# Splitting the load and the norm of x over two queues and two engines at the head of a one-core transformer block

## The chip, the cores and the metric

The kernel runs on one core of one Trainium2 chip. The metric is the device time of one execution in microseconds; the time of a kernel is the median of its runs.

## The reference, cut to what matters

The reference is one hybrid transformer layer over 256 tokens of width 1024 and a final norm: a state space mixer and a sparse attention side by side, then a mixture of 32 experts. Only its first lines matter here. A vector `c` gives shift and scale by a product with `w_ada`, the tokens `x` are normalized row by row, and the result goes into one wide projection:

```python
ada = jax.nn.silu(c) @ w_ada + b_ada
shift1, scale1, gate1, shift2, scale2, gate2 = [a[:, None, :] for a in jnp.split(ada, 6, axis=-1)]
hn = _rmsnorm(h, norm1_g) * (1.0 + scale1) + shift1     # x * rsqrt(mean(x * x) + eps) * g
... hn @ w_xbc, hn @ w_q, ...                             # w_in, 1024 x 9040
```

Everything is in float32.

## The kernel before

The work is one long program for the five engines, written stage by stage. A framework orders the instructions on each engine by its own estimate of when their inputs are ready, so the order on an engine can differ from that of the lines (in the timeline below, the load of x's first half stands ahead of the row loads that the program writes first).

**Loads.** All weights are a list, `stream`, issued in order on SyncE's queue (SP): for k = 0 to 7 first `ada{k}` (columns of `w_ada`, two transfers of 512 KB) and `sl{k}` (128 rows of `w_in`, 768 KB), then the rest. `slot` takes one of 19 buffers, `pump` issues as long as buffers are free, `release` gives one back.

**The front.** The tokens come in two halves of 128 rows, `Xv[:, 0]` and `Xv[:, 1]`, 512 KB each. `rows` loads `c`, `norm1_g` and `b_ada` as rows of a cleared tile `T1r`; TensorE turns it (L299) and ScalarE takes the columns (`th`, `T1`, L304, L305). GpSimd works out silu of c, `sc`. `warm` issues products that nobody reads: `WARM0` = 6 on the identity at the start and `WARM1` = 14 on `T1r` behind L299. One such product is two instructions in the trace.

**The norm.** The sums of squares of the two halves are formed on ScalarE (half 0, L331) and on VectorE (half 1, L328); both stand in `ssq`. A trial root on one element (L333) brings ScalarE's table for roots in early. `rsqrt` then treats both halves in one go: a root on ScalarE (L315), and on VectorE five small instructions (L316 to L320) that make the reciprocal and refine it. VectorE scales half 0 (L335), ScalarE half 1 (L336), into XN.

**The first projection.** For each k, `p0_rows` forms row k of shift and scale (16 instructions `ar<-ada,sc`), `p0_ab` turns it into columns, `xn_transposes` turns XN (four instructions for two k, L404, both halves of XN in each group) and copies it to XT, `p0_cols` makes the normalized input in two parts, HH and HL, `p0_split` makes the parts `wh` (ScalarE) and `wl` (VectorE) of the weight slice `sl{k}`, one half at a time, and `p0_mm` issues 18 products for each half. On TensorE the order is `p0_rows(0)`, `xn_transposes(0)`, four filling products on XT, `xn_transposes(1)`, `p0_mm(0, 0)`, and so on. Products of all helpers stand under L104 (`mm`), VectorE's under L87, L90, L94 and L95.

Of the kernel before, what the change touches and what calls it, by code (L numbers as in the profile page):

```python
# [12 lines left out]
AF = mybir.ActivationFunctionType  # L13
OP = mybir.AluOpType
# [4 lines left out]
D = 1024  # L19
# [3 lines left out]
EPS = 1e-6  # L23
# [5 lines left out]
WARM, WARMN = 1, 8  # L29
WN = 128  # L30
WARM0 = 6
WARM1 = 14
WARM2 = 1
WARM3 = 12
RATE_XB, RATE_ATTN, RATE_SSD = 1.15, 1.5, 1.35
# [22 lines left out]
def tile_hybrid_block(ctx: ExitStack, tc: tile.TileContext, x, c, positions, w_ada, b_ada, norm1_g, w_in, conv_w,  # L58
                      conv_b, dt_bias, a_log, d_skip, ssm_norm_g, w_ssm_out, cmp_pe_k, cmp_w1_k, cmp_w2_k, cmp_pe_v,
                      cmp_w1_v, cmp_w2_v, w_nsa_out, w_o, norm2_g, w_router_group, b_router_group, w_router_expert,  # L60
                      b_router_expert, w_exp_gate, w_exp_up, w_exp_down, final_g, out, dbg=None):
    nc = tc.nc
    PE, V, A, G, SP = nc.tensor, nc.vector, nc.scalar, nc.gpsimd, nc.sync
# [10 lines left out]
    def ps(b, name):  # L74
        return psp.tile([128, 512], F32, tag=f"b{b}", name=name)

    def work(shape, tag, name, bufs=1, dt=F32):
        return wk.tile(shape, dt, tag=tag, bufs=bufs, name=name)

    def const(shape, name, dt=F32):  # L80
        return csp.tile(shape, dt, name=name)

    def lasting(shape, name, dt=F32):
        return cst.tile(shape, dt, name=name)

    def stt(o, a, s, b, op0, op1):
        return V.scalar_tensor_tensor(o, a, s, b, op0=op0, op1=op1)  # L87

    def tt(o, a, b, op):
        return V.tensor_tensor(o, a, b, op=op)  # L90

    def ts(o, a, s1, op0, s2=None, op1=None):
        if op1 is None:
            return V.tensor_scalar(o, a, s1, None, op0=op0)  # L94
        return V.tensor_scalar(o, a, s1, s2, op0=op0, op1=op1)  # L95

    def warm(b, n):

        for _ in range(n):
            w = box["warm"]  # L100
            mm(b[:, 0:w.shape[1]], ident, w, True, True)
# [4 lines left out]
    def dram(ap, off, dims):  # L106
        return bass.AP(tensor=ap.tensor, offset=ap.offset + off, ap=dims)
# [14 lines left out]
    def slot(name):  # L122
        tag = free.pop(0)
        tag_of[name] = tag
        return (big if tag[0] == "s" else box["xtra"]).tile([128, 2048], F32, tag=tag, name=name)
# [11 lines left out]
    def keep(n):  # L137
        st["keep"] = n
        pump()
# [92 lines left out]
    T1r = work([128, 128], "w1k", "T1r", 4)  # L232
    V.memset(T1r, 0.0)

    def rows(q, dst, r0, src, n):
        q.dma_start(dst[r0:r0 + n, :], dram(src, 0, [[128, n], [1, 128]]))

    X = slot("X")
    Xv = X.rearrange("p (t d) -> p t d", t=2)
    rows(SP, T1r, 0, c, 8)  # L240
    rows(SP, T1r, 8, norm1_g, 8)
    rows(SP, T1r, 16, b_ada, 16)
    for i in range(2):
        SP.dma_start(Xv[:, i], x[0, i * 128:(i + 1) * 128, :])
    keep(4)


# [46 lines left out]
    epsc = lasting([128, 1], "epsc")  # L294
# [5 lines left out]
    box["warm"] = T1r  # L300
    warm(ps(6, "warm"), WARM1)
    T1 = const([128, 32], "T1")
    th = const([128, 8], "th")
# [8 lines left out]
    def rsqrt(o, ss, n, name):  # L312

        v, t = const([128, n], name + "v"), const([128, n], name + "t")
        A.activation(o, ss, AF.Sqrt, bias=epsc, scale=1.0 / D)  # L315
        ts(v, ss, 1.0 / D, OP.mult, EPS, OP.add)  # L316
        V.reciprocal(o, o)
        tt(t, o, o, OP.mult)
        stt(t, t, -0.5, v, OP.mult, OP.mult)
        stt(o, t, 1.5, o, OP.add, OP.mult)  # L320
# [1 line left out]

    XN = slot("XN")
    XNv = XN.rearrange("p (t d) -> p t d", t=2)
    ssq = const([128, 2], "ssq")
    for i in range(2):
        if i:
            V.tensor_tensor_reduce(out=XNv[:, i], in0=Xv[:, i], in1=Xv[:, i], scale=1.0, scalar=0.0, op0=OP.mult,  # L328
                                   op1=OP.add, accum_out=ssq[:, i:i + 1])
        else:  # L330
            A.activation(XNv[:, i], Xv[:, i], AF.Square, accum_out=ssq[:, i:i + 1])  # L331
    rx = const([128, 2], "rx")
    A.activation(rx[0:1, 0:1], th[0:1, 0:1], AF.Sqrt, scale=0.0, bias=epsc[0:1])  # L333
    rsqrt(rx, ssq, 2, "rx")
    ts(XNv[:, 0], Xv[:, 0], rx[:, 0:1], OP.mult)  # L335
    A.activation(XNv[:, 1], Xv[:, 1], AF.Copy, scale=rx[:, 1:2])  # L336
    XT = slot("XT")
    XTv = XT.rearrange("p (k t) -> p k t", k=8)
    HH, HL = slot("HH"), slot("HL")
# [1077 lines left out]
    def carve(t, *shapes):  # L1417

        at, r = 0, []
        for sh in shapes:  # L1420
            n = 1
            for k in sh:
                n *= k
            v, names = t[:, at:at + n], "abcde"[:len(sh)]
            at += n
            r.append(v.rearrange(f"p ({' '.join(names)}) -> p {' '.join(names)}",
                                 **dict(zip(names[1:], sh[1:]))) if len(sh) > 1 else v)
        return r
# [10 lines left out]
    hp, th, DTc, DTd = carve(scr2, (256,), (256,), (256,), (256,))  # L1439
# [396 lines left out]
    sf, vf, rf, rv, r_ = carve(rw_[:, 256:268], (2, 2), (2,), (2,), (2,), (2,))  # L1836
# [75 lines left out]
```

## Time and profile before

| | us |
|---|---|
| median of 3 runs | 681.53 |
| lowest and highest run | 680.92, 682.42 |
| the profiled execution | 683.83 |
| span of the profiled execution, first to last instruction | 682.1 |
| TensorE busy | 634.7 (93%) |
| VectorE busy | 468.3 (69%) |
| ScalarE busy | 324.7 (48%) |
| read from HBM | 190.98 MB |

Busy times are unions over the span; a matmul's end is modelled, so a busy TensorE is not one at its peak. In the rows further down, PE is TensorE's products, PEld its weight loads, DVE VectorE, ACT ScalarE, POOL GpSimd, SPq SyncE's queue of issues. A row of a timeline has the start, the duration, engine, line, operation, the tiles (written <- read), the shapes, a count, and in brackets the idle time before it and what ended it.

### The profile page before, as it was taken

The page shows a single profiled execution, that of the slowest core. Times are in us where ns is not written, and L with a number is a line of the kernel's source. Part 1 is how long each engine was busy: PE and PEld are TensorE (multiplying, and loading weights), DVE is VectorE, ACT ScalarE, POOL GpSimd, SP SyncE. Part 2 cuts the span into 40 slices and gives each one's busy share as a digit, 9 for nine tenths or more (in the row PEclk, how much of TensorE's full clock was granted, in tenths as well). Part 3 has the DMA queues.
Part 4 walks back from the last instruction along what each step waited for, and adds up shares of the span by engine and source line. Part 5 has one row for each costly group of instructions (what it writes and reads, how often), then busy time and mean ns, then how long its engine had stood idle before and what let it go on. Part 6 is the DMA issues. An engine that isn't in the chain of part 4 may idle for free. (4 is left out here: it accounts for less than half of the span.)

```text
span 682.1 us, 14140 instructions
## 1 busy us (share of the span) xinstructions
PE 634.7 (93%) x5610; PEld 500.9 (73%) x5611; DVE 468.3 (69%) x1158; ACT 324.7 (48%) x630; POOL 7.5 (1%) x67
## 2 busy tenths in 40 slices
PE   7999999899899999999999999998988999989873
PEld 6889889797767787898998999874646645655532
DVE  3657999995787878786899867565635634555635
ACT  4435878763358776463845544443223212223214
POOL 2000000000000000000000000000000000000000
PEclk9999999999989999999999999998998999999998
DMA  8997971478647767636395988656999999999992
GB/s 263 335 336 247 371 225 41 147 247 285 214 133 250 264 220 231 209 125 216 123 309 187 378 345 330 249 195 237 383 411 422 418 419 419 418 420 418 418 382 93
DMA packets 102196, 193.28 MB, mean 283 GB/s; under 512 B 7636, under 2 KB 83940, under 8 KB 90596
## 3 DMA queue, kind: packets, MB, share of 16 engines
q1 hardware_dynamic: 101268, 191.05, 77.4%
q8 instruction: 57, 0.93, 0.6%
q10 hardware_dynamic: 848, 1.11, 0.5%
q14 instruction: 23, 0.19, 0.1%
HBM read 190.98 MB, written 1.16 MB: 282 GB/s over the span
## 5 line engine op out<-in xcount | busy, mean ns | idle before, releaser
L104 PE MATMUL moe<-u,XG 128*32 128x256 f32 (+1 forms) x560 | 71.3, 381 | 3.3 <-SPq L1709 1.9
L104 PE MATMUL moe<-g,XG 128*32 128x256 f32 (+1 forms) x560 | 70.0, 380 | 2.5 <-PEq L1585 1.6
L104 PEld LDWEIGHTS moe<-g,XG 128*32 128x32 f32 (+1 forms) x560 | 38.3, 112 | 22.4 <-issue 10.0
L87 DVE SCALAR_TENSOR_TENSOR hp<-hp,moe 64x256 f32<-64x256 f32 x32 | 13.4, 419 | 47.0 <-ACT hp L1608 46.5
L104 PEld LDWEIGHTS moe<-u,XG 128*32 128x32 f32 (+1 forms) x560 | 35.7, 112 | 11.5 <-DMA u<-in_w_exp_up_dram 2.5
L104 PE MATMUL moe<-d,rw 128*32 128x512 f32 (+1 forms) x280 | 37.7, 617 | 2.0 <-ACT XG L1504 1.2
L1608 ACT ACTIVATE hp<-moe 64x256 f32<-64x256 f32 x32 | 12.1, 379 | 54.1 <-PEq L1585 31.3
L104 PE MATMUL pj_z<-HH,wl 128*128 128x256 f32 x128 | 37.1, 290 | 0.6 <-DVE wl L90 0.6
L104 PE MATMUL pj_z<-HH,wh 128*128 128x256 f32 x128 | 36.9, 288 | 0.0
L104 PE MATMUL pj_z<-HL,wh 128*128 128x256 f32 x128 | 36.7, 287 | 0.0
L104 PE MATMUL moe<-DT,HFh 128*128 128x256 f32 x128 | 32.0, 299 | 2.1 <-DVE DT L90 1.1
L1652 ACT ACTIVATE Y<-moe 128x512 fp32r<-128x512 f32 x15 | 9.0, 597 | 49.1 <-DVE moe L90 49.1
L913 ACT ACTIVATE P<-P,mn 128x128 f32<-128x128 f32 (+1 forms) x64 | 28.4, 446 | 5.4 <-DVE mn L910 5.3
L104 PE MATMUL moe<-DT,HFl 128*128 128x256 f32 x128 | 30.7, 289 | 0.2 <-DVE HFl L87 0.2
L1504 ACT ACTIVATE XG<-moe,GC 128x256 f32<-128x256 f32 x36 | 18.1, 564 | 25.6 <-PE moe L104 25.6
L104 PE MATMUL pj_xb<-HH,wh 128*128 128x256 f32 x96 | 27.0, 282 | 3.0 <-ACT BC L493 1.5
L104 PEld LDWEIGHTS moe<-DT,HFh 128*128 128x128 f32 x128 | 24.0, 196 | 5.8 <-issue 5.8
L104 PE MATMUL xa<-HH,wh 128*128 128x256 f32 x96 | 27.8, 293 | 0.0
L104 PE MATMUL pj_xb<-HH,wl 128*128 128x256 f32 x96 | 26.8, 279 | 0.0
L104 PE MATMUL pj_xb<-HL,wh 128*128 128x256 f32 x96 | 26.8, 279 | 0.0
L104 PEld LDWEIGHTS pj_z<-HH,wl 128*128 128x128 f32 x128 | 24.6, 192 | 2.9 <-issue 1.6
L104 PE MATMUL xa<-HL,wh 128*128 128x256 f32 x96 | 26.5, 280 | 0.0
(479 smaller groups left out, 2002.0 us busy)
## 6 DMA issues: line engine op xcount, KB each, us to landing
g<-in_w_exp_gate_dram SPq DMA_DIRECT2D x30, 1024.0 KB
u<-in_w_exp_up_dram SPq DMA_DIRECT2D x30, 1024.0 KB
d<-in_w_exp_down_dram SPq DMA_DIRECT2D x30, 1024.0 KB
ad<-in_w_ada_dram SPq DMA_DIRECT2D x16, 1024.0 KB
ada<-in_w_ada_dram SPq DMA_DIRECT2D x16, 512.0 KB
z<-in_w_in_dram SPq DMA_DIRECT2D x8, 1024.0 KB
so<-in_w_ssm_out_dram SPq DMA_DIRECT2D x8, 1024.0 KB
qk<-in_w_in_dram SPq DMA_DIRECT2D x8, 936.0 KB
```

The costliest lines, as they stand in the source:

```text
L87: return V.scalar_tensor_tensor(o, a, s, b, op0=op0, op1=op1)
L104: return PE.matmul(o, l, r, start=start, stop=stop)
L913: A.activation(o, o, AF.Exp, bias=mn[:, n:n + 1], scale=-1.0, accum_out=sm[:, n:n + 1])
L1504: A.activation(o, b_, AF.Identity, scale=GC[:, 1, k:k + 1], bias=GC[:, 0, k:k + 1])
L1608: A.activation(th[g], B4[g, s * 256:(s + 1) * 256], AF.Tanh, scale=0.5)
L1652: A.activation(R(Y[:, 0]), B6, AF.Copy)
```

## The change

The second half of x and the three row loads are issued by ScalarE's queue, x's first half stays on SP. Each half of x has a norm of its own: half 0 is squared and scaled by ScalarE; of half 1, ScalarE squares the first 512 columns and VectorE the others, an addition joins the sums, and VectorE scales the first 512 columns and ScalarE the others. `norm_of` is `rsqrt` for one column. The trial root covers two elements. `WARM1` goes from 14 to 9.

```diff
--- before.py
+++ after.py
@@ -29,7 +29,7 @@
 WARM, WARMN = 1, 8
 WN = 128
 WARM0 = 6
-WARM1 = 14
+WARM1 = 9
 WARM2 = 1
 WARM3 = 12
 RATE_XB, RATE_ATTN, RATE_SSD = 1.15, 1.5, 1.35
@@ -237,11 +237,11 @@
 
     X = slot("X")
     Xv = X.rearrange("p (t d) -> p t d", t=2)
-    rows(SP, T1r, 0, c, 8)
-    rows(SP, T1r, 8, norm1_g, 8)
-    rows(SP, T1r, 16, b_ada, 16)
-    for i in range(2):
-        SP.dma_start(Xv[:, i], x[0, i * 128:(i + 1) * 128, :])
+    SP.dma_start(Xv[:, 0], x[0, 0:128, :])
+    rows(A, T1r, 0, c, 8)
+    A.dma_start(Xv[:, 1], x[0, 128:256, :])
+    rows(A, T1r, 8, norm1_g, 8)
+    rows(A, T1r, 16, b_ada, 16)
     keep(4)
 
 
@@ -322,18 +322,29 @@
 
     XN = slot("XN")
     XNv = XN.rearrange("p (t d) -> p t d", t=2)
-    ssq = const([128, 2], "ssq")
-    for i in range(2):
-        if i:
-            V.tensor_tensor_reduce(out=XNv[:, i], in0=Xv[:, i], in1=Xv[:, i], scale=1.0, scalar=0.0, op0=OP.mult,
-                                   op1=OP.add, accum_out=ssq[:, i:i + 1])
-        else:
-            A.activation(XNv[:, i], Xv[:, i], AF.Square, accum_out=ssq[:, i:i + 1])
-    rx = const([128, 2], "rx")
-    A.activation(rx[0:1, 0:1], th[0:1, 0:1], AF.Sqrt, scale=0.0, bias=epsc[0:1])
-    rsqrt(rx, ssq, 2, "rx")
-    ts(XNv[:, 0], Xv[:, 0], rx[:, 0:1], OP.mult)
-    A.activation(XNv[:, 1], Xv[:, 1], AF.Copy, scale=rx[:, 1:2])
+    ssq, ssh = const([128, 2], "ssq"), const([128, 2], "ssh")
+    rx, rv, rt_ = const([128, 2], "rx"), const([128, 2], "rv"), const([128, 2], "rt_")
+
+    def norm_of(i):
+        o, v, t, q = (w[:, i:i + 1] for w in (rx, rv, rt_, ssq))
+        A.activation(o, q, AF.Sqrt, bias=epsc, scale=1.0 / D)
+        ts(v, q, 1.0 / D, OP.mult, EPS, OP.add)
+        V.reciprocal(o, o)
+        tt(t, o, o, OP.mult)
+        stt(t, t, -0.5, v, OP.mult, OP.mult)
+        stt(o, t, 1.5, o, OP.add, OP.mult)
+
+    A.activation(XNv[:, 0], Xv[:, 0], AF.Square, accum_out=ssq[:, 0:1])
+    A.activation(rx[0:1, 0:2], th[0:1, 0:2], AF.Sqrt, scale=0.0, bias=epsc[0:1])
+    norm_of(0)
+    A.activation(XNv[:, 0], Xv[:, 0], AF.Copy, scale=rx[:, 0:1])
+    A.activation(XNv[:, 1, 0:512], Xv[:, 1, 0:512], AF.Square, accum_out=ssh[:, 0:1])
+    V.tensor_tensor_reduce(out=XNv[:, 1, 512:1024], in0=Xv[:, 1, 512:1024], in1=Xv[:, 1, 512:1024], scale=1.0,
+                           scalar=0.0, op0=OP.mult, op1=OP.add, accum_out=ssh[:, 1:2])
+    tt(ssq[:, 1:2], ssh[:, 0:1], ssh[:, 1:2], OP.add)
+    norm_of(1)
+    ts(XNv[:, 1, 0:512], Xv[:, 1, 0:512], rx[:, 1:2], OP.mult)
+    A.activation(XNv[:, 1, 512:1024], Xv[:, 1, 512:1024], AF.Copy, scale=rx[:, 1:2])
     XT = slot("XT")
     XTv = XT.rearrange("p (k t) -> p k t", k=8)
     HH, HL = slot("HH"), slot("HL")
```

## Rows read from the trace of the kernel before

**Rows 1.** The page: busy tenths of TensorE and of the DMA engines in 40 slices of 17 us.

```profile
span 682.1 us, 14140 instructions
...
PE   7999999899899999999999999998988999989873
...
DMA  8997971478647767636395988656999999999992
```

**Rows 2.** [...]

```profile
1.00:2.00 1.00, 0.33 (x1) 0.33 (x2) 0.10 (x1) 1.00 (x1) 0.97 (x10) 1.00 0.51 41
2.00:3.00 1.00, 1.00 (x6) 1.00 (x6) 0.00 (x0) 0.12 (x1) 1.00 (x30) 1.00 0.63 233
3.00:4.00 1.00, 1.00 (x7) 1.00 (x7) 0.00 (x0) 0.00 (x0) 1.00 (x7) 1.00 0.85 288
4.00:5.00 1.00, 0.60 (x3) 0.30 (x2) 0.00 (x0) 0.43 (x1) 1.00 (x9) 1.00 0.41 142
5.00:6.00 1.00, 0.61 (x3) 0.64 (x4) 0.00 (x0) 0.86 (x4) 0.29 (x2) 1.00 0.76 238
6.00:7.00 1.00, 1.00 (x7) 1.00 (x6) 0.00 (x0) 0.98 (x3) 0.41 (x2) 1.00 0.94 269
...
16.60:60.00 43.40, 43.40 (x411) 38.28 (x411) 25.08 (x53) 17.40 (x25) 0.19 (x1) 1.00 1.02 312
...
75.00:78.00 3.00, 2.13 (x9) 1.33 (x8) 2.13 (x5) 2.66 (x5) 0.00 (x0) 1.00 1.05 381
...
184.60:191.40 6.80, 6.80 (x40) 5.41 (x40) 4.43 (x13) 1.17 (x5) 0.00 (x0) 0.50 0.48 156
```

**Rows 3.** The timeline of the front, all engines, from 0 to 17 us.

```profile
0.84 0.40 SPq L244 DMA_DIRECT2D X<-in_x_dram  x1
...
1.29 0.36 SPq L236 DMA_DIRECT2D T1r<-in_c_dram  x1
...
1.67 2.93 PE L104 MATMUL warm<-ident 128*128 128x128 f32 x12 [1.67 <-POOL ident L251]
...
2.39 0.42 SPq L244 DMA_DIRECT2D X<-in_x_dram  x1
2.85 1.57 SPq L156 DMA_DIRECT2D ada<-in_w_ada_dram  x2
...
4.57 1.06 ACT L331 ACTIVATE XN<-X 128x1024 f32<-128x1024 f32 x1 [2.46 <-DMA X<-in_x_dram]
...
5.39 0.44 PE L299 MATMUL cols<-ident,T1r 128*128 128x128 f32 x1 [0.79 <-DMA T1r<-in_b_ada_dram]
...
5.62 5.63 PE L104 MATMUL warm<-T1r,ident 128*128 128x128 f32 x28
...
7.45 0.29 ACT L333 ACTIVATE rx<-th,epsc 1x1 f32<-1x1 f32 x1
8.52 1.23 DVE L328 CUSTOM_DVE_ANT_0 XN<-X 128x1024 f32<-128x1024 f32 x1 [7.42 <-DMA X<-in_x_dram]
...
9.85 0.29 ACT L315 ACTIVATE rx<-ssq,epsc 128x2 f32<-128x2 f32 x1 [2.11 <-DVE ssq L328]
...
10.18 0.17 DVE L317 RECIPROCAL rx<-rx 128x2 f32<-128x2 f32 x1
...
10.97 1.15 ACT L336 ACTIVATE XN<-X,rx 128x1024 f32<-128x1024 f32 x1 [0.82 <-DVE rx L87]
10.97 0.75 DVE L94 TENSOR_SCALAR XN<-X,rx 128x1024 f32<-128x1024 f32 x1
...
12.56 1.07 PE L104 MATMUL ar<-ada,sc 128*32 128x256 f32 x16 [1.31 <-DMA ada<-in_w_ada_dram]
...
13.56 0.66 PE L404 MATMUL xa<-ident,XN 128*128 128x128 f32 x4
...
16.61 0.39 PE L104 MATMUL xa<-HH,wh 128*128 128x256 f32 x1
```

**Rows 4.** Instructions by tile: duration ns min/median/max, first and last start in us. The first is T1r from 5.6 to 10.2, the second T1r from 10.6 to 11.3, the third `ar` from 12 to 14 and the fourth `adr`, of the same form, from 188 to 190.3.

```profile
L104 PE MATMUL warm<-T1r,ident x22: 421/421/421, 5.6 to 10.1; 128*128 128x128 f32 x22
...
L104 PE MATMUL warm<-T1r,ident x6: 275/275/384, 10.3 to 11.0; 128*128 128x128 f32 x6
...
L104 PE MATMUL ar<-ada,sc x16: 376/379/403, 12.6 to 13.3; 128*32 128x256 f32 x16
...
L104 PE MATMUL adr<-ad,sc x16: 634/634/636, 188.5 to 189.8; 128*32 128x256 f32 x16
```

**Rows 5.** Timelines of ScalarE, VectorE and TensorE around 30 us: one weight slice on its way into the first projection.

```profile
30.61 0.85 ACT L227 ACTIVATE wh<-sl 128x768 fp32r<-128x768 f32 x1 [1.45 <-DMA sl<-in_w_in_dram]
...
31.48 0.96 DVE L90 TENSOR_TENSOR wl<-sl,wh 128x768 fp32r<-128x768 f32 x1 [1.31 <-ACT wh L227]
...
33.45 0.37 PE L104 MATMUL xa<-HH,wh 128*128 128x256 f32 x1
```

**Rows 6.** The timeline of the end of the kernel, where the same operations run on 512 columns.

```profile
673.07 0.60 ACT L1852 ACTIVATE SJ<-moe 128x512 f32<-128x512 f32 x1
673.57 0.19 ACT L1852 ACTIVATION_READ_ACCUMULATOR SJ<-moe 128x1 f32 x1
...
675.42 0.48 DVE L94 TENSOR_SCALAR OU<-OU,rw 128x512 f32<-128x512 f32 x1
...
676.21 0.70 ACT L1874 ACTIVATE OU<-OU,rw 128x512 f32<-128x512 f32 x1
```

## Prediction, made before the changed kernel ran

> **What bounds the kernel now.** I read the page first, for where the 682.1 us go [rows 1]: TensorE is busy in nine tenths or more of most slices, and the first slice is the emptiest but the last two. The change touches nothing behind the first 14 us, so two questions are left: when the first product can start, and whether the rest of the kernel moves with it. For the second I read busy time by stretch [rows 2]: from 16.6 to 60 us TensorE is busy 43.40 of 43.40 us, and the next idle stretch of note is 0.87 us between 75 and 78. Work in one gapless queue moves as a block if its inputs come in time. The inputs of the first projection are the `ada` and `sl` loads, and the DMA engines are full there too (share 1.02). So the margin of the supply matters [rows 5]: a slice of `sl` lands at 30.61 (ScalarE's wait on it ends), is rounded in 0.85, its remainder ready at 31.48 + 0.96 = 32.44, and TensorE takes the next half at 33.45. The margin is 1.0 us. A start earlier by more than that needs earlier loads as well.
>
> For the first question I followed the timeline of the front [rows 3]. Only SP issues loads: x's first half at 0.84, then the three row loads, x's second half at 2.39, and only at 2.85 the first `ada`. x's first half ends ScalarE's wait at 4.57; the second ends VectorE's at 8.52, though it has the same size and was issued 1.55 us later. From 8.52 runs one chain: squares 1.23, root at 9.85, the refinement from 10.18, both scaled halves from 10.97 to 12.12. The transposes of XN could start there, but stand behind the products `ar` on TensorE, which wait for the first `ada` until 12.56 and last to 13.56. So two late arrivals meet at the same place: XN at 12.12 and `ada` at 12.56 plus 1.0. The transposes start at 13.56, the first real product at 16.61.
>
> **Part by part: the loads.** SP loses four issues in front of the first `ada`: 2.85 becomes about 1.29, a lead of 1.56. ScalarE's queue takes four issues of about 0.4 each, some 1.6 us from 0.84, while ScalarE waits for x anyway until 4.57; they cost it nothing (without that cover, 1.6). The row loads also wait for T1r's clearing; the tool that orders instructions put x ahead of them on SP for that, so I expect x's second half in front on ScalarE's queue too.
> The bytes are the same. DMA shares of 0.63, 0.85, 0.41, 0.76 and 0.94 between 2 and 7 us [rows 2] add to 3.59, where five full microseconds at 1.02 would be 5.1: 1.5 us of transfer time are unused, 0.6 of it in the dip at 4 to 5, behind the short row loads. Two queues in parallel should fill most of it, not the ramp before 4 (0.56). So all loads behind x come earlier by 0.95 to 1.56 us; below, nothing, if the dip has another cause. I take 1.2: the first `ada` at 11.36, `ar` done 1.0 later, at 12.36. The supply's margin grows to 1.0 + 1.2 = 2.2, above what I ask of it.
> [...] That x's second half, whose bytes need 1.7 us at 312 GB/s, takes four after the first is no matter of issuing time alone.
>
> **When x is there.** Both halves are 1.05 MB. By 4.0 us the engines had moved 41 + 233 + 288 KB = 0.56 MB [rows 2]; the rest at 312 GB/s takes 1.6 us, so 5.6 for both if they share evenly. The first half, until now alone at 4.57, then comes between 4.57 and 5.6; I take 5.0, a loss of 0.4. The second gains 2.9.
>
> **The norm.** From the start of the first squares to the end of the trial root is 7.74 - 4.57 = 3.17 on ScalarE now (squares, small columns, table load, root) [rows 3]; from 5.0 that is 8.17. Root of half 0: 0.29, to 8.46. Refinement up to the scaled copy: from 10.14 to 10.97 now, 0.83, to 9.29. Copy of half 0 on ScalarE: 1.15, to 10.44. ScalarE idles during those 0.83, and the squares of 512 columns fit in: 0.60 and a reading of 0.19 [rows 6]. VectorE's half of the squares, about half of 1.23, runs from 5.6 on, beside the table load. Then root of half 1, 0.29, behind the copy: 10.73; refinement 0.83: 11.56; the two quarters at once, 0.70 on ScalarE and 0.48 on VectorE [rows 6]: 12.26. XN is thus done no earlier than now (12.12): six more small VectorE instructions and the serial second chain eat what the second half's landing gives. If the ordering leaves the squares behind the copy, 0.8 more and the addition 0.16: 13.2. If it puts the second root ahead of the copy, the copy is the longer way: about 11.3.
> The gate is the later of 12.36 and 12.26: transposes at 12.36 instead of 13.56, a gain of **1.2**; bounds 0.35 (13.2) and 2.1 (x at 4.57, root ahead, `ada` earlier by 1.56 and the dip's 0.6).
>
> **The warm products.** Before, 28 instructions at a pace of 0.213 (22 of them from 5.6 to 10.1 [rows 4]) hold TensorE to 11.25. With 9 pairs there are 18: from about 5.6 with the row loads at 5.4 as now, 18 x 0.213 = 3.8, so to 9.5. They cost nothing, as `ar` comes at 11.36. Fourteen pairs at the low pace would last to 11.6 and hold `ar` by 0.2. Their price lies in the clock, below.
>
> **The sum.** 1.2 us less at the first transposes, carried through the gapless stretch: 683.83 - 1.2 = 682.6 for the profiled execution. That one lies 2.3 above the median of the runs (its span 682.1, and 1.7 around it); against the median, 681.53 - 1.2 = **680.3**.
>
> **Rival 1, the clock (slower).** The granted-clock column shows 1.00 in the first 10 us [rows 2], but durations contradict it: the warm products took 421 ns until 10.1 and 275 from 10.3 to 11.0, and the same form as `ar` takes 379 at a granted 1.00 and, as `adr`, 634 where 0.50 is granted [rows 2, 4]. [...] The new run is 3.9 us long and then idles for 1.9. If the clock has not risen by then, `ar` takes about 1.9 instead of 1.07 (+0.85), two groups of transposes 0.45 more each, the eight filling products behind XT 0.5 beyond what HH hides: 2.25 us, and each product until the rise another 0.1. That gives 680.3 + 2.25 to 3.5, about 683.0; it decides if the clock is still low when `ar` starts, for what is saved is then spent twice. Against it: 4 us of work is near what came before the rise.
> [...]
>
> **Rival 2, the halves come late or out of order.** x's first half, sharing the engines, lands at 5.6, or the squares stay behind the copy: XN at about 13.2, gain 0.35, 681.2. For it: VectorE's and ScalarE's queues are in order, and the second root waits behind a 1.15 copy. Against: ScalarE's squares already stand ahead of the small columns that the program writes first, so the order follows readiness.
>
> **Rival 3, more than I ask.** The stall between x's halves disappears altogether, `ada` comes 2 us earlier and the second root overtakes the copy: gain 2.1, 679.4; beyond that the supply's margin ends it.
>
> **How the numbers follow.** Forecast 0.52 (its own range 679.7 to 681.0, by gains of 1.8 and 0.5), clock 0.17, late halves 0.18, more 0.13. Runs of this kernel spread from 680.92 to 682.42, so about 0.2% (1.4 us) is what a measurement can tell: the bounds are 680.2 and 682.9. Below lie all of "more" and somewhat under half of the forecast: 0.13 + 0.23 = 0.36. Above lies two thirds of the clock case: 0.12, rounded up. The rest is 0.52. The range 679.0 to 682.9 leaves out the upper half of the clock case and a little of "more", about 0.12.
>
> **What would show it.** In the new profile: first `ada` issue near 1.3 on SP; VectorE's squares near 5.6 instead of 8.52; `ar` near 11.4 and the transposes near 12.4; the first product near 15.4; after that the same order, all 1.2 earlier, with no new wait on `sl`. Wrong if `ar` still starts at 12.5 (the loads did not gain), if the scaling of half 1 ends past 13 (the chain), or if `ar` takes 634 ns instead of 379 (the clock).

## The result, and the profile of the changed kernel

The changed kernel takes 686.44 us (median of 20 runs, 683.52 to 691.41) against 682.51 us before (20 runs, 679.88 to 687.04): ratio 1.0068, 95% interval 1.0048 to 1.0089. It is **slower** by 0.7%, above the range of the prediction. The ratios here are those on record of fast runs alone, so this one differs a little from the quotient of the two medians (1.0058), and that of a_9_17 further down leaves out three slow runs of 690.0 to 691.0 us.

The timeline of the front, changed kernel, the lines that answer to [rows 3]; columns: start, length, engine, line, operation, out<-in, and in brackets the idle time before it and what ended it:

```profile
0.84 0.39 SPq L240 DMA_DIRECT2D X<-in_x_dram  x1
0.84 0.41 ACTq L242 DMA_DIRECT2D X<-in_x_dram  x1
1.29 1.05 SPq L156 DMA_DIRECT2D ada<-in_w_ada_dram  x2
...
2.21 0.41 ACTq L236 DMA_DIRECT2D T1r<-in_b_ada_dram  x1
...
5.93 1.06 ACT L337 ACTIVATE XN<-X 128x1024 f32<-128x1024 f32 x1 [2.00 <-DMA X<-in_x_dram]
...
6.20 0.69 DVE L342 CUSTOM_DVE_ANT_0 XN<-X 128x512 f32<-128x512 f32 x1 [5.10 <-DMA X<-in_x_dram]
...
8.51 0.45 PE L299 MATMUL cols<-ident,T1r 128*128 128x128 f32 x1 [3.91 <-DMA T1r<-in_b_ada_dram]
...
8.75 4.05 PE L104 MATMUL warm<-T1r,ident 128*128 128x128 f32 x18
9.00 0.18 ACT L304 ACTIVATE th<-cols 128x8 f32<-128x8 f32 x1 [1.30 <-PE cols L299]
...
10.57 0.29 ACT L338 ACTIVATE rx<-th,epsc 1x2 f32<-1x2 f32 x1
10.90 0.48 ACT L330 ACTIVATE rx<-ssq,epsc 128x1 f32<-128x1 f32 x2
...
12.01 1.15 ACT L340 ACTIVATE XN<-X,rx 128x1024 f32<-128x1024 f32 x1 [0.63 <-DVE rx L87]
...
12.90 1.80 PE L104 MATMUL ar<-ada,sc 128*32 128x256 f32 x16
13.06 0.71 ACT L347 ACTIVATE XN<-X,rx 128x512 f32<-128x512 f32 x1
...
15.34 0.58 PE L104 MATMUL ac<-ones,rw 128*128 128x1 f32 x4 [0.64 <-DVE rw L369]
...
15.77 0.63 PE L415 MATMUL xa<-ident,XN 128*128 128x128 f32 x4
...
19.40 0.52 PE L104 MATMUL xa<-HH,wh 128*128 128x256 f32 x1
```

The issues came as predicted (`ada` at 1.29), and x's second half is there at 6.20 instead of 8.52. But the row loads, now on ScalarE's queue and there behind x's second half, arrive at 8.51 instead of 5.39, and three things stand behind T1r: the small columns, for which ScalarE waits 1.30 us and which come ahead of the roots (trial root at 10.57 instead of 7.45); the warm products (to 12.80, all behind a late start); and behind those `ar`. The first product comes at 19.40 instead of 16.61, 2.8 us late. The span grew by 2.8 too (684.9 against 682.1), so the front looks like the whole answer. The experiments show that it isn't, and the two traces agree with them. The changed kernel is 3.5 us behind at the end of the first projection (63 us), but only 0.7 at the end of the last projection ahead of the router (products `wo_p`, 446 us): before's execution runs 6.8 us at a granted 0.50 from 184.6 ([rows 2], where the granted clock stands ahead of the DMA engines' share and the GB/s, and 1.00 is full speed), the changed kernel's 3.4, from 185.1. Then it falls back to 2.0 at the first pair of experts and to 2.6 at the last, so the two 2.8 are equal by chance.

### The profile page after: what moved, and what is told of

The parts are those of the page before. It is cut to its first block, busy times and chain, and to the rows that moved or that the text cites. A ratio compares the mean times of both kernels' runs of the same rounds, so it can differ in the third digit from the quotient of the medians.

```text
span 684.9 us, 14125 instructions
## 1 busy us (share of the span) xinstructions
PE 634.7 (93%) x5600; PEld 500.2 (73%) x5601; DVE 467.9 (68%) x1164; ACT 323.3 (47%) x632; POOL 7.5 (1%) x67
## 3 DMA queue, kind: packets, MB, share of 16 engines
HBM read 190.98 MB, written 1.16 MB: 281 GB/s over the span
## 5 line engine op out<-in xcount | busy, mean ns | idle before, releaser
L104 PE MATMUL moe<-u,XG 128*32 128x256 f32 (+1 forms) x560 | 69.4, 380 | 0.0
L104 PEld LDWEIGHTS moe<-g,XG 128*32 128x32 f32 (+1 forms) x560 | 39.8, 112 | 25.1 <-issue 8.1
L104 PE MATMUL moe<-d,rw 128*32 128x512 f32 (+1 forms) x280 | 39.6, 648 | 2.0 <-ACT XG L1515 1.2
L1619 ACT ACTIVATE hp<-moe 64x256 f32<-64x256 f32 x32 | 12.1, 379 | 51.5 <-PEq L1596 31.4
L104 PE MATMUL moe<-Y,DT 64*128 64x512 f32 x120 | 18.6, 422 | 10.5 <-PEq L1596 8.6
```

The source lines that it names most:

```text
L104: return PE.matmul(o, l, r, start=start, stop=stop)
L1619: A.activation(th[g], B4[g, s * 256:(s + 1) * 256], AF.Tanh, scale=0.5)
```

## Experiments

### Which part of the change costs: loads, rows or warm pairs

**a_rows_sp**, the changed kernel with the row loads back on SyncE's queue (written ahead of x, and issued as before, behind x's first half):

```
-    SP.dma_start(Xv[:, 0], x[0, 0:128, :])
-    rows(A, T1r, 0, c, 8) ...
+    rows(SP, T1r, 0, c, 8); rows(SP, T1r, 8, norm1_g, 8); rows(SP, T1r, 16, b_ada, 16)
+    SP.dma_start(Xv[:, 0], x[0, 0:128, :])
     A.dma_start(Xv[:, 1], x[0, 128:256, :])
```

> The changed kernel with one thing undone: the three row loads (c, norm1_g, b_ada) go out on SP behind x's first half again; x's second half stays on ScalarE's queue, the split norm and 9 warm pairs stay. Theory 'late rows' (T1r came at 8.5 us instead of 5.4, and the column instruction, the warm products and the trial root all hang on it): T1r by 6.2, trial root done by 9, first real product near 16.3, time about 682 to 683. Rival 'clock' (9 pairs are too few, whenever they run): T1r is early but `ar` still takes about 634 ns and the time stays at 685 or above. Rival 'norm' (the split norm is the longer chain): XN done past 13 although T1r is early.

**a_rows_first**, rows ahead of x's second half on ScalarE's queue (a write of one column of x's buffer by VectorE, which the load overwrites, keeps it behind them):

```
     SP.dma_start(Xv[:, 0], x[0, 0:128, :])
+    V.memset(Xv[:, 1, 0:1], 0.0)
     rows(A, T1r, 0, c, 8)
-    A.dma_start(Xv[:, 1], x[0, 128:256, :])
     rows(A, T1r, 8, norm1_g, 8)
     rows(A, T1r, 16, b_ada, 16)
+    A.dma_start(Xv[:, 1], x[0, 128:256, :])
```

> The changed kernel with the three row loads ahead of x's second half on ScalarE's queue (one small clearing of x's second half makes its load wait until the rows are issued). Theory 'late rows': T1r by 5.5 and the front as with the rows on SP, SP free for `ada` at 1.29 besides; 681.5 to 683. Rival 'clock': `ar` at 634 ns, 685 or above. If T1r still comes past 8, being behind x's second half was not what delayed it, but ScalarE's queue itself.

**a_warm14**, the changed kernel with the old number of pairs:

```
-WARM1 = 9
+WARM1 = 14
```

> The changed kernel with 14 warm pairs instead of 9, all else as changed. Theory 'late rows': T1r still at 8.5, the warm products hold TensorE to about 14.2, the first product no earlier than in the changed kernel (19.4) but at the high clock: 685 to 687. Rival 'clock': the whole loss is the missing products, the time returns to 682 to 683.

**b_warm9**, the kernel before with the new number and nothing else:

```
-WARM1 = 14
+WARM1 = 9
```

> The kernel before with 9 warm pairs instead of 14, nothing else. Theory 'late rows': the products end at about 9.5 and `ar` waits for `ada` until 12.5 anyway; a loss of at most 1.5 where the clock comes late: 682.5 to 684. Rival 'clock': `ar` at 634 ns and a loss of 3 or more, 685.5 or above.

| kernel | median us | ratio to before, 95% | first product us |
|---|---|---|---|
| a_rows_sp | 687.76 | 1.0069 (1.0037 to 1.0101) | 16.25 |
| a_rows_first | 688.00 | 1.0066 (1.0036 to 1.0097) | 19.89 |
| a_warm14 | 682.44 | 0.9988 (0.9965 to 1.0011) | 18.78 |
| b_warm9 | 686.84 | 1.0064 (1.0032 to 1.0095) | 16.42 |

The four kernels with 9 pairs (the change among them) lose two thirds of a per cent, whatever their loads and their norm; a_warm14, with 14, loses nothing. The late rows are not the cause: a_rows_sp starts its first product 0.36 us ahead of before and is as slow as the change, a_warm14 starts it 2.2 us behind and is as fast as before. The loss comes with the five pairs. Their count isn't all that differs: the framework orders by its estimates, so in b_warm9 two transposes of the front stand elsewhere than before, and in a_warm14 the products of the second projection (`qkp`) stand in another order than in the change. But in b_warm9's profiled front `ar` takes 379 ns, as in before, and the first product comes at 16.42 against before's 16.61, so in that execution the loss arises elsewhere. a_rows_first also answers a question of its own: its row loads are issued ahead of x's second half on ScalarE's queue and still come at 8.45, so being behind it was not what made them late.

### Where: the expert stage, by its place in TensorE's stream

In the expert stage TensorE takes pairs of experts under `tc.If` (L1585 is a branch of `either`). The program numbers its 16 pairs from 0, and so does this text. With 9 pairs of warm products the step from the 9th to the 10th pair of experts (start of `moe<-d,rw`) took 11.5 us in the changed kernel and 12.05 in b_warm9, against 9.16 before. Theory: five pairs fewer move all later instructions of TensorE forward in its stream, and so the places where it waits for its own instructions. Two runs test it. Each differs by five late products alone from a kernel above (b_14_7 from before, b_9_17 from b_warm9), with the work of VectorE, ScalarE, GpSimd and SyncE in the same order.

**b_14_7**: the kernel before, its front untouched, fewer of the products in front of the router's choice, just ahead of the expert stage.

```
-WARM3 = 12
+WARM3 = 7
```

> The kernel before with its 14 pairs in front, and 7 instead of 12 warm products in front of the router's choice. The front is word for word that of before; only the expert stage and what follows stand five products earlier in TensorE's stream. 'Position': slower as with 9 pairs in front, ratio 1.004 to 1.009, the last expert product near 667, with the long stall between the 9th and 10th expert pair. 'Front': no change, 0.998 to 1.002 (the five products lie in a wait of TensorE for the router's choice).

**b_9_17**: nine pairs in front, and the expert stage back at its old place.

```
-WARM1 = 14
+WARM1 = 9
-WARM3 = 12
+WARM3 = 17
```

> The kernel before with 9 pairs of warm products in front instead of 14, and 17 instead of 12 in front of the router's choice, where the expert stage begins: TensorE's stream is shorter by five products up to that place and as long as before's behind it. Theory 'position' (the number of instructions that stand ahead of the expert stage in TensorE's stream decides where that stage stalls on its branches): ratio to before within 0.9975 to 1.002, the last expert product near 664.5 as in before, no stall over 2 us at the branch near 603. Rival 'front' (9 pairs in front leave something behind that costs later: clock, order, phase of the loads): as with 9 pairs alone, 1.0064 (1.004 to 1.009).

b_14_7: 684.79 us, **1.0034** (1.0012 to 1.0057). An untouched front, five products fewer just ahead of a wait of TensorE, and the kernel is slower, though by less than 'position' foresaw (1.004). b_9_17: 684.46 us, 1.0036 (1.0010 to 1.0063): its step of the 9th to the 10th pair is 9.25 again, but the time is not, and it lies between the two theories' ranges. The late products lie in that wait only in part: from the last start of `wo_p` to the first expert product it is 17.4 us with 12 of them (before), 17.0 with 7 (a_14_7, c_14_7) and 17.9 with 17 (b_14_17).

TensorE's timeline there, kernel before:

```profile
603.74 0.39 PE L104 MATMUL moe<-u,XG 128*32 128x256 f32 x2
604.71 1.20 PE L104 MATMUL moe<-Y,DT 64*128 64x512 f32 x8 [0.58 <-PEq L1585]
606.48 0.45 PE L1627 MATMUL moe<-ident,hp 64*128 64x64 f32 x2 [0.58 <-DVE hp L87]
606.93 0.66 PE L104 MATMUL moe<-ident,DW 128*64 128x128 f32 x8
607.52 1.92 PE L104 MATMUL moe<-d,rw 128*32 128x512 f32 x16
```

The same place in b_14_7:

```profile
600.67 0.39 PE L104 MATMUL moe<-u,XG 128*32 128x256 f32 x2
603.68 2.07 PE L104 MATMUL moe<-Y,DT 64*128 64x512 f32 x8 [2.62 <-PEq L1585]
605.90 0.47 PE L1627 MATMUL moe<-ident,hp 64*128 64x64 f32 x2
606.30 1.12 PE L104 MATMUL moe<-ident,DW 128*64 128x128 f32 x8
607.35 3.27 PE L104 MATMUL moe<-d,rw 128*32 128x512 f32 x16
```

The wait for TensorE's own sequencer (PEq) behind the branch is 2.62 us instead of 0.58, and what follows is slower: `moe<-Y,DT` takes 2.07 us instead of 1.20, `moe<-d,rw` 3.27 instead of 1.92. The granted clock is 0.50 from 603.3 to 610.1. So the wait is paid twice, once as a wait and once as a lower clock. What TensorE waits for shows in the DMA view: the queue q8 carries instructions. Two stretches of b_14_7, from 600.9 to 602.2 and from 602.2 to 603.7 (queue, kind: packets, MB, share of 16 engines):

```profile
q1 hardware_dynamic: 74, 0.52, 97.2%
q8 instruction: 1, 0.02, 5.2%
...
q1 hardware_dynamic: 82, 0.63, 100.1%
```

One packet of 16 KB, which starts at 601.0 and takes 1.08 us, at the very moment when TensorE runs dry (its last product ends at 601.06), while expert weights fill the engines. In the kernel before, the packet of the same place lies in the stretch from 602.0 to 603.3, and none from 603.3 to 604.7:

```profile
q1 hardware_dynamic: 69, 0.52, 98.7%
q8 instruction: 1, 0.02, 5.2%
...
q1 hardware_dynamic: 81, 0.57, 97.8%
```

It starts at 602.1, two microseconds before the products end at 604.1, and most of it is hidden behind them. Over the profiles of all kernels, those with five products fewer ahead of this place (after twice, a_rows_sp, a_rows_first, b_warm9 twice, b_14_7, a_14_7, c_14_7) have 11.5 to 12.4 us from the 9th to the 10th pair, the others (11 profiles) 9.0 to 9.3. No profile stands on the wrong side, though the five products are taken away far in front in some and just ahead of the experts in others.

That TensorE waits here for instructions can be read from the times of packets and products. In all twenty profiles the products behind this branch start 2.62 to 2.69 us after the start of that packet. In the nine it starts within 0.2 us of the moment when TensorE runs dry, and the wait is 2.50 to 2.81; in the eleven it starts 1.97 to 2.22 us earlier, and the wait is 0.43 to 0.67. Other places show the same: between 466 and 668 us the twenty profiles have 77 waits over 0.9 us that the profile puts to TensorE's sequencer, and all of them end 2.5 to 3.0 us behind the start of a 16 KB packet. So how much of the wait work covers depends on where the packet falls, and that moves with the place in the stream. What fills the 1.6 us between the packet's landing and the next product, the profile does not show.

From the first pair's `moe<-d,rw` to the end of the last pair's, the nine profiles take 200.3 us in the mean (198.1 to 202.0) and the eleven 197.7 (195.8 to 200.4). Of these 2.6 us, 1.4 are waits of TensorE; the rest lies in products, with 15.3 us at a granted 0.50 against 8.3. Not every step is longer: that from pair 2 to pair 3 takes 15.0 against 17.0.

In before q8 moved 57 packets and 0.93 MB, 16 KB each. How many instructions a packet holds is not shown, so neither is the share of one that the ten products and ten weight loads make up which `WARM1` lost.

The weights are not what is late. SyncE's issues of the last expert loads, before:

```profile
653.82 4.15 SPq L171 DMA_DIRECT2D d<-in_w_exp_down_dram  x4
```

and in b_14_7:

```profile
652.19 4.11 SPq L171 DMA_DIRECT2D d<-in_w_exp_down_dram  x4
```

The loads are 1.6 us earlier in b_14_7, yet its last pair starts at 668.65 against 667.86: TensorE lost 2.4 us on the way against its supply. It is 2.1 us ahead of before at the end of `wo_p`, 2.0 at the first pair, 3.3 at the 9th and 0.2 at the 10th.

**b_14_17**, the kernel before with five products more in front of the router:

```
-WARM3 = 12
+WARM3 = 17
```

> The kernel before with 14 pairs in front and 17 instead of 12 warm products in front of the router's choice: the expert stage stands five products later in TensorE's stream than in before, where the other runs had it five earlier. 'Position': another set of long waits on TensorE's sequencer between the expert pairs than either before or the shorter kernels have; the ratio can go either way (0.995 to 1.006), the sign is not known beforehand. 'Fewer products cost, more do not' (the five are useful as work in front of the router): the same waits as before, 0.998 to 1.002.

683.24 us, 1.0012 (0.9986 to 1.0037): no loss that can be measured. Its 9th to 10th pair is 9.14 apart, but a wait of 1.4 us stands at 521.6 where before has none over 0.6: other waits, about the same sum (12.1 us of gaps over 0.6 us behind 466 us, 11.6 before, 14.2 in b_14_7). The ratio lies in the ranges of both theories and does not part them.

### Is it the same in the changed kernel

**a_14_7** and **a_9_17** on the changed kernel, **c_14_7** and **c_9_17** on a_rows_sp, each with one of two edits:

```
14_7:  WARM1 = 9 -> 14, WARM3 = 12 -> 7
9_17:  WARM3 = 12 -> 17
```

'Two parts' takes the loss for the sum of two: a front at a granted 0.50, and the place of the expert stage in TensorE's stream. For a_9_17 it foresaw 1.002 to 1.005, with the expert pairs as in before (9th to 10th near 9.2 us apart).

> The changed kernel with 14 pairs in front (ratio 0.9988 so far) and 7 instead of 12 warm products in front of the router's choice; all else in the same order. 'Two parts': the place's price comes back alone, 1.001 to 1.005, with the 9th to 10th pair near 12 us apart. 'Place alone': 1.004 to 1.009. 'Front alone': 0.997 to 1.001, and no change between the expert pairs.

> The changed kernel with its 9 pairs, and 17 instead of 12 warm products in front of the router's choice; all else in the same order. [...] 'Place alone': 0.998 to 1.001. 'Front alone': 1.005 to 1.009, as the change itself.

> The changed kernel with the row loads on SP's queue, 14 pairs in front and 7 late products: expert stage five products earlier. 'Place alone': the whole loss comes back without any change in front, 1.0055 to 1.009, 9th to 10th expert pair 11.5 to 12.4 us apart. 'Two parts': 1.002 to 1.005 with the same expert pairs.

> The changed kernel with the row loads on SP's queue, 9 pairs in front and 17 late products: expert stage at before's place. 'Place alone': the whole loss of 1.0069 goes, 0.997 to 1.0015, and the 9th to 10th expert pair 9.1 to 9.3 us apart. 'Two parts': 1.002 to 1.005 with the same expert pairs.

And the partner of c, **a_rows_sp_warm14**, a_rows_sp with `WARM1 = 14`:

> The changed kernel with the row loads back on SP's queue and 14 pairs. With 9 pairs this kernel had its first product 0.36 us ahead of before and ended 4.6 us behind it. 'Position': the expert stage runs as in before, and what is gained in front arrives at the end: 0.9965 to 1.000, the last expert product near 664. 'Front' (14 pairs keep the clock or the phase right): also no loss, so this run does not part the two; it tells whether the start's gain is kept to the end, by the first product (16.3 or a little later) and the last expert product.

| base | 9 pairs, 12 late | 14 pairs, 12 late | 14 pairs, 7 late | 9 pairs, 17 late |
|---|---|---|---|---|
| before | 1.0064 | 1 | 1.0034 (1.0012 to 1.0057) | 1.0036 (1.0010 to 1.0063) |
| change | 1.0068 | 0.9988 | 1.0072 (1.0047 to 1.0096) | 1.0010 (0.9976 to 1.0045) |
| change, rows on SP | 1.0069 | 0.9994 (0.9969 to 1.0019) | 1.0058 (1.0036 to 1.0080) | 1.0052 (1.0028 to 1.0076) |

The third column is settled: five late products fewer cost in all three, between 0.34 and 0.84% against the kernel to its left, and the place is what the profiles show for it. The fourth is not: the expert stage runs as in before in each (9.2 us), but two of three kernels are still slower. (The runs of a_9_17 lie in three heaps, 680 to 682, 685 to 686 and 690 to 691. The median of all is 685.34, 1.0057 times that of before, so its 1.0010 is not firm.) "Place alone" holds for a_14_7 and c_14_7 and falls with c_9_17; "two parts" holds for the row of before and nearly for c_9_17 (1.0052 against 1.005), and fell with a_14_7. So the place is one cause, and 9 pairs have a second, less regular one. In c_9_17's profile that one lies ahead of the experts: it is 0.5 us ahead of before at the end of `wo_p` and 2.6 behind at the first pair.

The windows show it: start and end, length, busy us and instructions of TensorE, granted clock, share of the DMA engines, GB/s. Before:

```profile
440.00:470.00 30.00, 25.90 (x205) 1.00 0.45 154
...
600.00:615.00 15.00, 13.34 (x176) 1.00 1.01 419
...
640.00:672.00 32.00, 23.37 (x246) 1.00 0.81 325
```

The same stretches in c_14_7:

```profile
440.00:470.00 30.00, 25.02 (x197) 1.00 0.45 155
...
600.00:615.00 15.00, 11.86 (x131) 0.77 1.01 419
...
640.00:672.00 32.00, 25.33 (x256) 0.95 0.77 309
```

In c_9_17:

```profile
440.00:470.00 30.00, 28.84 (x205) 0.89 0.42 150
...
600.00:615.00 15.00, 13.31 (x170) 1.00 1.01 420
...
640.00:672.00 32.00, 23.86 (x248) 1.00 0.88 356
```

In the changed kernel:

```profile
440.00:470.00 30.00, 27.73 (x205) 0.94 0.44 150
...
600.00:615.00 15.00, 11.77 (x143) 0.89 1.01 419
...
640.00:672.00 32.00, 26.29 (x256) 0.89 0.83 332
```

With the expert stage five products early, the clock falls between 600 and 615, in all nine profiles and in none of the other eleven. Behind 650 it falls in all nine too, but also in five of the eleven (a_warm14, b_14_17, b_9_17, a_w0_11, a_rows_sp_warm14). In c_9_17 it falls between 453 and 460, in front of the experts, where the products ahead of the router slow down (TensorE's timeline of c_9_17):

```profile
451.45 5.57 PE L104 MATMUL warmr<-Yo,ident 128*128 128x72 f32 x34 [0.51 <-DVE Yo L87]
```

In b_14_17 the same 34 take 4.01. From `wo_p`'s last start to the first expert product c_9_17 needs 20.6 us where b_14_17 needs 17.9. The fall is in a_9_17's profile and b_9_17's first too, not in b_9_17's second; the wait ahead of it is 0.51 us in all. Half as long (3.4 us), it is in both profiles of the changed kernel and in b_14_7, which has 14 pairs, but not in a_rows_sp, a_rows_first and b_warm9. In all, 5 of 13 profiles with 9 pairs have it and 1 of 7 with 14. Why it falls there stays open.

### The front's clock

**b_warm9_look**, **b_9_17_look** and **after_look** are one more execution each of programs above, with its profile.

> The kernel before with 9 pairs, a second look. Its first profile had the warm products at the low pace until 9.56, `ar` at 379 ns and the first product at 16.42; the kernel with the same front and 17 late products had them at the high pace until 7.1 and 7.6, then 4 us of idleness, a clock of 0.50 from 12 us on and the first product at 19.73 and 18.87. 'Clock by chance of its phase': this look may show either; where the warm products end before 8, the first product comes after 18. 'Fixed by the program': 16.42 again.

> A second look at the kernel before with nine pairs in front and 17 late products, whose first profile had `ar` at 634 ns and the first product at 19.73, although its front is word for word that of the kernel with nine pairs alone, whose profile had 379 ns and 16.42. 'Clock by chance': this look may show either; a front at 379 ns and a first product near 16.4 would show that the same instructions run at either level. 'Fixed by the program': 634 ns and 19.7 again.

> The changed kernel, a second look. 'Two parts': the expert pairs as in its first profile (9th to 10th near 11.5 us apart), for their order of instructions is fixed; its front may run at either clock (first product between 17 and 20).

TensorE's timeline in b_warm9, first profile:

```profile
6.23 3.61 PE L104 MATMUL warm<-T1r,ident 128*128 128x128 f32 x18
11.54 1.07 PE L104 MATMUL ar<-ada,sc 128*32 128x256 f32 x16 [1.70 <-DMA ada<-in_w_ada_dram]
...
16.42 0.39 PE L104 MATMUL xa<-HH,wh 128*128 128x256 f32 x1
```

and in the second:

```profile
5.50 2.17 PE L104 MATMUL warm<-T1r,ident 128*128 128x128 f32 x18
11.83 1.94 PE L104 MATMUL ar<-ada,sc 128*32 128x256 f32 x16 [4.16 <-DMA ada<-in_w_ada_dram]
...
19.50 0.52 PE L104 MATMUL xa<-HH,wh 128*128 128x256 f32 x1
```

One program, two fronts 3.1 us apart. In the second the 18 products are through in 2.17 us, TensorE idles 4.16 us for `ada`, and what follows up to the first product is slow: `ar` takes 1.94 us and the eight products on XT 2.07. In the first the 18 last 3.61 us, the wait is 1.70, and `ar` takes 1.07, the eight 1.16. b_9_17's two profiles have the first product at 19.73 and 18.87. The first products of three profiles with 14 pairs and before's front came at 16.27 to 17.04. The latest of them, b_14_17's, shows the same in small: there a granted 1.00 is on record from 4.7, the 28 instructions are through in 3.29 us, TensorE idles 3.10, and the clock is back at 0.50 from 11.5 to 14.9. after_look repeats the changed kernel: first product at 19.29, the 9th to 10th pair 12.1 apart.

**a_w0_11**, **b_w0_11** and **c_w0_11** put the five pairs back in the first warm group, which needs no load in the changed kernel, in the one before, and in a_rows_sp. The order in the projections changes with it in all three. 'Position and clock' takes the five pairs to have two separate prices: the place of the expert stage in TensorE's stream, and a front that in some executions stays at a granted 0.50. For c_w0_11 it foresaw that neither is paid: first product at 16.0 or earlier, 0.996 to 1.000.

```
-WARM0 = 6
+WARM0 = 11
 WARM1 = 9
```

> The changed kernel with 11 instead of 6 warm products of the first group (which need no load) and its 9 pairs of the second: as many instructions as 14 pairs, and the same start of the second group at 8.75. 'Position': the loss goes, 0.997 to 1.001, as with 14 pairs of the second group (0.9988). 'Front': the second group is still 9 pairs, so the loss stays, 1.005 to 1.009.

> The kernel before with 11 products in the first warm group and 9 pairs in the second: the same number of instructions as before everywhere behind, the same nine pairs as in the kernel with 17 late ones (1.0036). 'Position and clock': neither is paid, 0.998 to 1.002, `ar` at 376 to 403 ns. 'Nine pairs as such' (the second group alone decides): 1.002 to 1.005, `ar` at 634 ns in the profile or the first product later than 17.

> The changed kernel with the row loads back on SP's queue and 11 instead of 6 products in the first warm group (which needs no load): before's number of instructions ahead of the expert stage, an early T1r, and a first group long enough to raise the clock. [...] Rival 'the start's gain is lost on the way': ratio 0.999 to 1.002 although the first product is 0.6 us earlier.

a_w0_11: 682.17 us, 0.9993 (0.9968 to 1.0018): the loss goes, with 9 pairs in the second group and first product at 16.11. b_w0_11: 685.45 us, **1.0041** (1.0017 to 1.0066), against expectation: `ar` runs at 379 ns at 11.74, then the clock falls from 13.7 to 20.5 us and the first product comes at 18.28. It is 1.7 us behind before at the first product and 5.3 at 151 us, so more than half of that is lost in the projections, whose order differs too; its loss isn't pinned to the front. c_w0_11: 683.01 us, 1.0011 (0.9982 to 1.0039), with the earliest front of all, in its TensorE timeline:

```profile
9.87 1.07 PE L104 MATMUL ar<-ada,sc 128*32 128x256 f32 x16 [0.73 <-DMA ada<-in_w_ada_dram]
...
15.20 0.39 PE L104 MATMUL xa<-HH,wh 128*128 128x256 f32 x1
```

The profiled execution spans 678.7 us, but its runs give no gain. No kernel beat the one before beyond its interval.

## Why the prediction was wrong, step by step

- **Baseline**: the forecast starts from a median of three runs, 681.53, and takes their spread of 0.2% for the noise. Twenty runs give 682.51 and spread from 679.88 to 687.04, so 1.0 us of the miss of 6.1 lies there.
- **Loads**: right in direction, size not settled. In the changed kernel `ada` was issued at 1.29 as foreseen, but TensorE took it late, so its landing doesn't show. In c_w0_11, where it is issued at 2.40 behind the rows, it ended TensorE's wait at 9.87, 2.7 us before [rows 3]'s 12.56, where I took 1.2 and at most 1.56. But eight profiles with before's loads have that wait end at 11.54 to 12.56: the one trace I read was the latest of them, and the lead is 1.7 to 2.7. x's first half came at 5.93, beyond my bounds (5.6), the second at 6.20.
- **Row loads "at 5.4 as now"**: failed. 8.51 in the changed kernel, 7.08 in a_rows_sp, where SP issues them as before and only x's second half and `ada` come earlier beside them. In the changed kernel the DMA engines are at a share of 0.97 to 1.28 in each microsecond from 3 to 9, where before had 0.85 and 0.41 in the two from 3 to 5 [rows 2], ahead of T1r's arrival. The term missed was what the short loads lose beside 1 MB of x and the `ada` loads that now come with it; that the full engines are the cause is an estimate from these shares and times. On ScalarE's queue they come later still, ahead of x's second half too (8.45 in a_rows_first); whether the queue does that or `ada`, issued at 1.29 there, is open.
- **Norm chain**: each instruction took what I took (1.06, 0.29, 1.15, 0.71), the order was better than feared (VectorE's half at 6.20, both roots ahead of the copy at 10.90), but the roots wait behind the columns of T1r. XN was done at 13.77, not 12.26, past the bound of 13.2 that rival 2 gave for another reason.
- **Transposes at 12.4**: 15.77, since `ar` ran from 12.90 for 1.80 us behind late warm products, and `ac` now stands ahead of the transposes in TensorE's order.
- **Rival 1, the clock**: the right subject and side. In the changed kernel its front came true: the 18 warm instructions took 421 ns each, `ar` 634 ns (1.80 us in all, it took 1.9), and the first record of a granted 1.00 starts at 14.43 (in before at 10.5). That was not fixed by the program: a_9_17 has the same front, and there `ar` took 379 ns and the first product came at 17.63. With before's front, nine pairs went slow another way than the rival feared: in b_warm9's second profile the 18 instructions were fast (2.17 us) and `ar` slow (1.94 us) behind the wait of 4.16 us that they leave, and the first product came 3.1 us late, inside its price of 2.25 to 3.5. But this front isn't what the runs lose: b_warm9's first profile has a fast front and the same loss behind it, and a_warm14 is 2.2 us late and loses nothing.
- **The step that failed**: "The change touches nothing behind the first 14 us", and with it that the warm pairs "cost nothing". Five pairs fewer moved every later instruction in TensorE's stream, and the instruction packets that it waits for in the expert stage, 600 us later, fell where no work covers them. Five products fewer just ahead of the experts cost 0.34 to 0.84% with 14 pairs in front, where the change costs 0.68%. A second part, which comes with nine pairs in some kernels and lies ahead of the experts, is not explained.
- **"Work in one gapless queue moves as a block"**: held for the stretch that was read. What a start is late or early it still is at the end of the first projection, 63 us: a_warm14 2.2 us late and 2.2, c_w0_11 1.4 early and 1.3, b_warm9 0.2 early and 0.2. Behind that it is not kept. In the four kernels with the rows on SP and 6 products in the first warm group, 0.3 to 0.6 ahead at 63 us becomes 1.7 to 1.9 behind at 151, over projections that run in another order than before's; and stretches at a granted 0.50 come at other places in each execution. At the end a_warm14's late start is no loss and c_w0_11's early one no gain, within intervals of 0.25% (1.7 us).

## What to carry to other kernels

Where an engine's program branches and comes in pieces, as here in packets of 16 KB, removing or adding instructions early is not local: test such an edit once with the count made up elsewhere, before its own effect is judged. Products that only keep an engine busy had two more effects here than the time they take: when they ended set the wait behind them (4.16 or 1.70 us in b_warm9's two profiles), after which products were slow or not (`ar` 1.94 or 1.07 us), and how many there were set where later packets fell. And short loads that a first step waits for should not be moved next to long ones on the ground that their issue is early: here they came at 8.51 instead of 5.39.

## What the runs showed of the hardware

- Instructions come through the DMA engines: q8 carries 57 packets of 16 KB, one every 3 to 26 us in before, about 1.07 us each in the expert stage, where the weights hold the engines at a share of 1.01. Behind the branches of that stage TensorE goes on 2.5 to 3.0 us after such a packet starts (77 waits over 0.9 us in twenty profiles).
- The same products ahead of the same wait ran at two paces in two executions of one program (2.17 and 3.61 us for 18), and the faster ones made the front slower by 3.1 us.
- Runs of one kernel spread over 4 to 8 us in most cases; the stretches at 0.50 (6.8 us at 184.6 in before [rows 2]) come at other places or not at all in other executions.
